# A fused transformer step in FP32: x loaded in natural rows, side work moved to other steps, other groups in the down projection

## Chip, core and metric

The kernel runs on one core of a Trainium2 chip. The metric is the device time of one execution in microseconds (us); the time of a version is the median of its runs.

## What is computed

One layer of a backbone for 512 latent tokens (a grid of 8 rows by 64 columns) and 128 context tokens, model width 2048, all in FP32. Cut to what matters here:

```python
sh1, sc1, g1, sh2, sc2, g2 = adaln(cond, w_ada, b_ada)       # silu(cond) @ w_ada: 2048 x 12288
h = modulate(rms_norm(x, norm1_g), sh1, sc1)
q, k, v, u = mixer_inputs(h, w_in, q_g, k_g)                  # one projection, 2048 x 4096
attn = neighbourhood_attention(q, k, v, cache_k, cache_v, rpb) # context tokens: dense attention
pool = multiscale_pool(u, w_pool, pool_scale)
x = x + g1 * merge_project(attn, pool, oa_g, op_g, w_out)     # 2048 x 2048
h = modulate(rms_norm(x, norm2_g), sh2, sc2)
x = x + g2 * swiglu(h, w_gate, w_up, w_down)                  # 2048 x 5632 twice, 5632 x 2048
```

Outputs are both kinds of tokens after the layer, and the context's new keys and values.

## The kernel before

**Layout.** The 640 tokens (latent first, then context) lie along the free dimension, features along the partitions. Inside the kernel the latent tokens are ordered by grid column, the 8 rows of a column next to each other. Every FP32 product is three matmuls of split operands: a value is `hi` (rounded for the fast FP32 mode) plus `lo` (the rest), and hi·hi, hi·lo and lo·hi are added.

**Start (to L683).** Five tiles of 128 tokens are loaded token by token (L259); `token_ap` gathers the latent ones in column order, so that neighbouring partitions are 64 tokens apart in memory. ScalarE (ACT) squares each tile, and VectorE (DVE) scales it. `turn` transposes one column block of 128 features on TensorE (PE) into PSUM, whence ACT writes `h_hi` and DVE `h`; GpSimd (POOL) makes `h_lo`. Meanwhile the value part of the input projection runs in blocks of one or two such column blocks, `starts`, in ten groups of matmuls each. The shift and scale of the first modulation are worked out beside it: `ada_stream` is a generator that loads a 1 MB piece of `w_ada` and multiplies it each time it is called; `next(stream)` after a group calls it once, `ada_until(b)` until block b is done. It has three buffers.

**Steps.** All other projections are cut into 688 steps. In a step a 256 x 256 tile of weights is multiplied by seven products in place of eight (a Strassen-like scheme of sums of quarters): 21 matmuls of 320 or 322 columns, into seven PSUM banks. `step` (L410) issues, for step s: `fetch(s+4)`, the weights' DMA on SyncE's queue (SP), into one of three buffers; `sums(s+3)`, the quarters' sums, on POOL; `x_hi(s+2)` on ACT and `x_lo(s+2)` on DVE, the split; then the jobs that `at((s, 0), ...)` registered for the step, the 21 matmuls (`products`), and the jobs of `(s, 1)`. At the end of a block `combine` (L397) adds the seven banks into an output tile: one copy on ACT (L401), seven additions on DVE (L400). The engines' queues run in program order, so a job stands ahead of all that is issued after it. In the last step of a block the split of step s+2 stands behind `combine`.

**Output projection.** 8 blocks of 8 steps. `x2_block` adds the gated result to x (DVE), stores it (SP) and sums its squares (ACT, POOL); `h2_block` scales it for the second norm (ACT) and stores it; `x_load` fetches the next x. The last block and the first gate block are ordered by a planner.

**Gate and up.** 22 pairs of 256 features, each a gate block and an up block of 8 steps. After a gate block: `scale_rho` (DVE, L1642), `gate` (ACT Silu, L1647). After an up block: `scale_rho`, `add_shift` (ACT), `times` (DVE, L1630), `f_sums` (DVE), and `f_split`, which splits seven operand tiles (ACT L1670, DVE L1671) and stores them to DRAM (`yh_s`, `yl_s`): four sums in step 3 after the block and three given quarters in step 6. Over the first nine blocks `ada_gen` works out the last modulation: groups of matmuls in steps 0 and 4, its transposes (L753) one step after ACT's copy (L749).

**Down.** The 22 pairs are taken in `GROUPS`, and within a group all 8 output blocks run, one step per pair; a result is added to `acc` in SBUF after each block (`accumulate`, DVE, L1769). The operands of a group are loaded back by `y_load` (four DMAs a pair, L1699) into 7 places; `late_loads` loads those whose place is not free before the group's last block. `start_sum` loads x for the sums. In the last group `finish` transposes two output blocks (PE, L1781) into one PSUM bank, copies and stores them; `finish_end` does the last two blocks behind the last step.

## Time and profile before

| | us |
|---|---|
| median of three runs | 2852.61 (2847.11 to 2853.16) |
| the profiled execution | 2848.62 |
| its span | 2846.8 |
| PE busy | 2628.8 (92%) |
| POOL busy | 1892.4 (66%) |
| DVE busy | 1872.0 (66%) |
| ACT busy | 1084.7 (38%) |

The span is the time from the first to the last event of the profiled execution. Busy times of engines overlap. A view of windows lists, for each stretch, the busy time of each engine with its count of instructions, the granted clock of PE as a share of full speed, the share of the DMA engines and the rate. In a list of instructions the brackets tell how long the engine was idle before one, and what ended that.

### The profile page before, as it was taken

To read this page: it belongs to the slowest core of one execution; us is meant where nothing else is said; L and a number is where in the kernel's file an instruction comes from. 1 tells how busy PE (TensorE), PEld (TensorE's weight loads), DVE (VectorE), ACT (ScalarE), POOL (GpSimd) and SP (SyncE) were. 2 spreads that over 40 slices of the span, in tenths; PEclk is the share of its full clock that TensorE was granted. 3 is DMA by queue.
4 is the path that set the end of the run, shared out by engine and by line. 5 is a ranking of instruction groups with operands and counts; after the bars stand their busy time and mean duration, and the time that the engine had idled before them with its cause. 6 is when DMAs were issued, how large, how long until landed. Compare 5 with 4: busy or idle time off the path is not lost. (4 is left out here: it accounts for less than half of the span.)

```text
span 2846.8 us, 46427 instructions
## 1 busy us (share of the span) xinstructions
PE 2628.8 (92%) x16968; PEld 2437.1 (86%) x16968; DVE 1872.0 (66%) x2580; ACT 1084.7 (38%) x1603; POOL 1892.4 (66%) x2265
## 2 busy tenths in 40 slices
PE   4997999988869977999999999999999989999998
PEld 2476988887668877888999999999999889998998
DVE  2469443458875587666676776776766778776765
ACT  3233222246633434434344444444444423332333
POOL 1257656567667867666677777676767568786764
PEclk9998999989989988999999999999999999999999
DMA  9922777768335443565344343343443765636343
GB/s 246 349 90 92 243 261 259 255 188 242 97 116 192 139 145 114 180 213 164 113 133 130 113 142 118 114 147 114 133 128 111 274 233 186 207 109 221 132 146 109
DMA packets 365142, 476.69 MB, mean 167 GB/s; under 512 B 22000, under 2 KB 286960, under 8 KB 364272
## 3 DMA queue, kind: packets, MB, share of 16 engines
q1 hardware_dynamic: 362752, 469.78, 50.9%
q10 hardware_dynamic: 2160, 3.93, 0.4%
q8 instruction: 133, 2.18, 0.3%
q14 instruction: 97, 0.79, 0.1%
HBM read 389.09 MB, written 84.54 MB: 166 GB/s over the span
## 5 line engine op out<-in xcount | busy, mean ns | idle before, releaser
L320 POOL TENSOR_TENSOR wf<-wf 128x128 f32<-128x128 f32 (+1 forms) x2007 | 1564.2, 786 | 670.6 <-DMA wf<-in_w_gate_dram 128.3
L393 PE MATMUL pp<-yhi,xhi 128*128 128x322 f32 (+1 forms) x4076 | 1285.8, 315 | 35.4 <-ACT c L401 14.9
L395 PE MATMUL pp<-yhi,xlo 128*128 128x322 f32 (+1 forms) x4076 | 1282.8, 315 | 23.7 <-DVE xlo L335 19.4
L394 PE MATMUL pp<-ylo,xhi 128*128 128x322 f32 (+1 forms) x4076 | 1273.4, 312 | 24.5 <-DMA ylo<-yl_s 10.0
L335 DVE TENSOR_TENSOR xlo<-wf,xhi 128x896 fp32r<-128x896 f32 x678 | 808.4, 1202 | 702.0 <-ACT xhi L329 669.7
L329 ACT CAST xhi<-wf 128x896 fp32r<-128x896 f32 x688 | 646.0, 941 | 1093.6 <-POOL wf L320 934.9
L393 PEld LDWEIGHTS pp<-yhi,xhi 128*128 128x128 f32 x4076 | 778.7, 191 | 67.1 <-DVE c L400 18.6
L395 PEld LDWEIGHTS pp<-yhi,xlo 128*128 128x128 f32 x4076 | 778.4, 191 | 40.2 <-DVE xlo L335 36.0
L394 PEld LDWEIGHTS pp<-ylo,xhi 128*128 128x128 f32 x4076 | 778.3, 191 | 27.2 <-DMA ylo<-yl_s 11.3
L400 DVE TENSOR_TENSOR c<-c,pp 128x320 f32<-128x320 f32 (+1 forms) x714 | 312.1, 484 | 85.3 <-ACT c L401 57.2
L393 PE MATMUL pp<-hhi,xhi 128*128 128x320 f32 x384 | 124.8, 325 | 0.2 <-DVE v L674 0.2
L394 PE MATMUL pp<-hlo,xhi 128*128 128x320 f32 x384 | 121.4, 316 | 0.0
L395 PE MATMUL pp<-hhi,xlo 128*128 128x320 f32 x384 | 121.4, 316 | 0.0
L394 PE MATMUL pp<-tlo,xhi 128*128 128x320 f32 x288 | 92.5, 321 | 16.7 <-DVE tlo L637 16.7
L393 PE MATMUL pp<-thi,xhi 128*128 128x320 f32 x288 | 91.2, 317 | 1.3 <-DVE v L674 1.3
L674 DVE TENSOR_TENSOR v<-g,v 128x512 f32<-128x512 f32 x80 | 54.9, 688 | 56.9 <-PE g L166 56.9
L395 PE MATMUL pp<-thi,xlo 128*128 128x320 f32 x288 | 91.5, 318 | 0.0
L393 PEld LDWEIGHTS pp<-hhi,xhi 128*128 128x128 f32 x384 | 74.6, 194 | 19.1 <-issue 13.4
L160 POOL TENSOR_TENSOR wlo<-raw,whi 128x512 fp32r<-128x512 f32 x32 | 41.3, 1312 | 69.9 <-ACT whi L159 68.3
L1671 DVE TENSOR_TENSOR c<-c,yh 128x640 f32<-128x640 f32 x88 | 82.3, 975 | 0.0
L1626 ACT ACTIVATE c<-c 128x320 f32<-128x320 f32 x132 | 50.6, 462 | 75.5 <-DVE c L1642 75.4
L1647 ACT ACTIVATE c<-c 128x320 f32<-128x320 f32 x132 | 52.9, 464 | 66.5 <-DVE c L1642 66.5
(238 smaller groups left out, 2586.5 us busy)
## 6 DMA issues: line engine op xcount, KB each, us to landing
araw<-in_w_ada_dram SPq DMA_DIRECT2D x60, 1024.0 KB, 6.7
wf<-in_w_gate_dram SPq DMA_DIRECT2D x176, 256.0 KB, 2.8
wf<-in_w_up_dram SPq DMA_DIRECT2D x176, 256.0 KB, 3.0
wf<-in_w_down_dram SPq DMA_DIRECT2D x176, 256.0 KB, 2.8
araw<-in_w_ada_dram SPq DMA_DIRECT2D x56, 512.0 KB, 7.0
wf<-in_w_in_dram SPq DMA_DIRECT2D x96, 256.0 KB, 4.3
yl_s<-c SPq DMA_DIRECT2D x66, 320.0 KB, 4.3
wf<-in_w_out_dram SPq DMA_DIRECT2D x64, 256.0 KB, 3.0
```

What stands on the lines that cost most here:

```text
L160: nc.gpsimd.tensor_tensor(lo, raw, hi.bitcast(F32), op=ALU.subtract)
L320: tt = lambda o, a, b, op: eng.tensor_tensor(o, a, b, op=op)
L329: nc.scalar.copy(hi, raws[s][:, 0:7, :])
L335: eng.tensor_tensor(lo, f[:, 0:7, :], hi.bitcast(F32), op=ALU.subtract)
L393: mm(b, lhsT=x[0][:, i, :], rhs=y[j][0], start=first, stop=False)
L394: mm(b, lhsT=x[0][:, i, :], rhs=y[j][1], start=False, stop=False)
L395: mm(b, lhsT=x[1][:, i, :], rhs=y[j][0], start=False, stop=last)
L400: add = lambda o, a, b: nc.vector.tensor_tensor(o, a, b, op=ALU.add)
L674: nc.vector.tensor_tensor(dst, ps, dst, op=ALU.add)
L1626: nc.scalar.activation(cq[:, c0:c1], cq[:, c0:c1], AF.Identity, bias=b)
L1647: nc.scalar.activation(cq[:, c0:c1], cq[:, c0:c1], AF.Silu, bias=b)
L1671: nc.vector.tensor_tensor(v, v, hi.bitcast(F32), op=ALU.subtract)
```

## The change

`x` is loaded in natural rows, and the reordering of tokens is done by the reading side of `turn`. All start blocks have two column blocks; the modulation stream is called from the first block on. In the output projection the two tiles of `x2_block` are handled in two steps, `h2_block` comes two steps later, and `x_load` one. In gate/up the gate's `scale_rho` and Silus come one step later, `f_split` works on one tile at a time (sums in step 3, given quarters in steps 9 and 10, that is 1 and 2 of the next up block), and the modulation generator runs in steps 2 and 6. The down groups have 4, 5, 4, 5, 4 pairs, loads and accumulations have other steps, and the ends of the last blocks are written anew. The core of the diff:

```diff
-    nc.sync.dma_start(c_s, c4)          # now behind the first ada_until
-    def turn(kt):
+    def turn(kt, eng=nc.gpsimd):
+        by_column = lambda v: v.rearrange("p (c r) -> p c r", r=ROWS)
...
+            if s == 0:
+                src = ps_s.rearrange("p (r c) -> p c r", r=ROWS)
+                to = [by_column(v[:, 0:SMP]) for v in (hi, h)]
+            else:
+                src, to = ps_p, [v[:, SMP:TOK] for v in (hi, h)]
+            nc.scalar.activation(to[0], src, AF.Identity, bias=b, scale=g)
+            nc.vector.tensor_scalar(to[1], src, g, b, op0=ALU.mult, op1=ALU.add)
-    starts = [(0, 1), (1, 1)] + [(k, 2) for k in range(2, NKT, 2)]
+    starts = [(k, 2) for k in range(0, NKT, 2)]
-        nc.sync.dma_start(xn[t], token_ap(x_sample, x_prompt, t, 0, D))
+        nc.sync.dma_start(xn[t], x_prompt if t == NT - 1 else x_sample[t * P : (t + 1) * P, :])
-    GROUPS = ((0, 3), (3, 7), (7, 12), (12, 17), (17, 22))
+    GROUPS = ((0, 4), (4, 9), (9, 13), (13, 18), (18, 22))
     turn(0)
+    turn(1, nc.vector)
-                if b:
-                    next(stream, None)
+                next(stream, None)
...
     def x2_block(j, c):
         for q in range(2):
-            x2_add(j, c, q)
-            nc.sync.dma_start(x2_s[2 * j + q], c[q][:, 0:TOK])
-        for q in range(2):
+            at((now[0] + q, 0), x2_tile, j, c, q)
+    def x2_tile(j, c, q):
+        x2_add(j, c, q)
+        at((now[0], 1), lambda: nc.sync.dma_start(x2_s[2 * j + q], c[q][:, 0:TOK]))
...
-            if n == 3:
+            if n == 4:
                 x_load(j)
-        at((now[0], 0), x2_block, j, c)
+        x2_block(j, c)
         if j < 6:
-            at((now[0] + 2, 0), h2_block, j, c)
+            at((now[0] + 4, 0), h2_block, j, c)
...
+    def f_split(pair, first, v):
+        n = v.shape[1]
+        hi = rhop.tile([P, 2, HB], F32R, tag="yh", name="yh", bufs=2)[:, 0:n, :]
+        nc.scalar.copy(hi, v)
+        nc.vector.tensor_tensor(v, v, hi.bitcast(F32), op=ALU.subtract)
...
-            at((first + 1 + 2 * i // 3, 1), y_load, p, part)
+            at((first + 1 + max(3 * i // 5, i // 4), 1), y_load, p, part)
...
-                    if ada_gen is not None:
-                        run_at(ada_gen, n % 4 == 0)
+                    if ada_gen is not None and n % 4 == 2:
+                        next(ada_gen, None)
-                at((now[0] + 3, 0), split_f_sums, sg, pair)
-                at((now[0] + 6, 0), split_f_given, c, pair)
+                later = 4 if pair == NPAIR - 1 else 9
+                for i in range(2):
+                    at((now[0] + 3, i), split_f_sums, sg, pair, i)
+                    at((now[0] + later + i, 0), split_f_given, c, pair, i)
-                at((now[0], 0), scale_rho, sg)
-                at((now[0], 1), gate, sg, 0)
-                at((now[0] + 1, 1), gate, sg, 1)
+                at((now[0] + 1, 0), scale_rho, sg)
+                at((now[0] + 1, 1), gate, sg, 0)
+                at((now[0] + 2, 1), gate, sg, 1)
...
-                at((now[0], 0), accumulate, j, c)
+                at((now[0] + (2 if gi == 0 else 0), 0), accumulate, j, c)
-            if last_group and j % 2 and j < 7:
+            if last_group and j in (1, 3, 5, 6):
                 for t in range(NT):
-                    at((now[0] + 2 + t, 1), finish, j - 1, t)
-    finish_end(6)
-    accumulate(7, c)
-    finish_end(7)
+                    at((now[0] + 1 + (t > 1), 1) if j == 6 else (now[0] + 2 + t, 1), finish, (j - 1, j)[j == 6 :], t)
+    finish_end(7, ps)
```

The new `finish_end` takes the seven banks in the order in which the last step fills them (0, 6, 1, 2, 4, 3, 5), adds, gates and accumulates quarter by quarter on DVE, and sends the five output tiles over SP's and ACT's queues. In the first group the early loads begin at step 8 and `start_sum` two to five steps later than before.

## Rows read from the trace of the kernel before

**Rows 1.** Windows, two stages: length; each engine's busy time, count; clock, DMA share, GB/s.

```profile
1108.40:2248.20 1139.80, 1116.87 (x7370) 1079.77 (x7370) 781.21 (x948) 482.19 (x733) 796.38 (x1027) 0.99 0.44 141
2248.20:2836.40 588.20, 561.48 (x3759) 554.37 (x3759) 421.38 (x627) 193.82 (x240) 408.58 (x523) 0.98 0.52 175
```

**Rows 2.** Windows, two stretches of the start, same columns.

```profile
45.00:50.00 5.00, 5.00 (x24) 3.57 (x26) 0.00 (x0) 2.92 (x6) 0.19 (x1) 1.00 0.01 2
50.00:147.00 97.00, 86.22 (x486) 43.82 (x474) 39.02 (x75) 20.48 (x37) 25.88 (x19) 0.98 1.04 337
```

**Rows 3.** Waits of PE: who waited for whom: us in total, times, longest.

```profile
PE pp L395 <- DVE xlo L335: 19.4, 25, 3.5
PE pp L394 <- DMA ylo<-yl_s: 10.0, 5, 3.1
PE pp L393 <- DVE c L400: 9.8, 23, 1.3
PE x L753 <- ACT rest L749: 9.2, 4, 2.6
```

**Rows 4.** Timeline of ACT, 0 to 29 us: start, length, what, idle before.

```profile
18.95 1.91 ACT L265 ACTIVATE junk<-x 128x2048 bf16<-128x2048 f32 x1 [3.50 <-DMA x<-in_x_sample_dram]
23.77 1.91 ACT L265 ACTIVATE junk<-x 128x2048 bf16<-128x2048 f32 x1 [2.82 <-DMA x<-in_x_sample_dram]
26.23 1.91 ACT L265 ACTIVATE junk<-x 128x2048 bf16<-128x2048 f32 x1 [0.45 <-DMA x<-in_x_prompt_dram]
```

**Rows 5.** Timeline of PE: the last modulation matmuls of the start.

```profile
145.92 1.07 PE L203 MATMUL acc<-araw,c 128*32 128x512 f32 x8
```

**Rows 6.** Groups of DVE instructions: count; busy us, mean ns; idle before.

```profile
L239 DVE TENSOR_SCALAR c<-ps_s,gs,sh 128x512 f32<-128x512 f32 x16 | 13.0, 809 | 23.9 <-ACT hhi L238 20.9 <-POOL wlo L160 1.9 <-POOL hlo L240 1.1
L219 DVE TENSOR_REDUCE red<-tr 128x8 f32<-128x32 f32 x7 | 1.3, 181 | 0.0
L219 DVE TENSOR_REDUCE red<-tr 128x4 f32<-128x16 f32 x2 | 0.3, 174 | 17.2 <-PE tr L217 17.2
```

**Rows 7.** Timeline of POOL in the output projection: two additions of squares.

```profile
902.82 3.20 POOL L1502 TENSOR_TENSOR c<-c,xT 128x640 f32<-128x640 f32 x2 [1.66 <-ACT xT L1501]
```

**Rows 8.** Windows: an up block, the shortest block, the last 34 blocks.

```profile
1494.61:1520.63 26.02, 25.70 (x171) 24.89 (x169) 16.16 (x23) 10.94 (x16) 21.21 (x28) 1.00 0.41 128
1935.05:1959.93 24.88, 24.88 (x171) 24.86 (x169) 18.64 (x23) 11.38 (x18) 15.68 (x21) 1.00 0.40 127
1366.95:2248.17 881.22, 868.18 (x5715) 849.01 (x5713) 621.02 (x747) 379.50 (x577) 634.49 (x811) 1.00 0.41 132
```

**Rows 9.** Timeline of DVE around the ends of an up and a gate block.

```profile
1467.44 3.20 DVE L400 TENSOR_TENSOR c<-c,pp 128x322 f32<-128x322 f32 x7 [0.58 <-ACT c L401]
...
1492.94 1.76 DVE L1671 TENSOR_TENSOR c<-c,yh 128x640 f32<-128x640 f32 x2
1494.62 3.19 DVE L400 TENSOR_TENSOR c<-c,pp 128x322 f32<-128x322 f32 x7
...
1500.44 1.55 DVE L1642 TENSOR_TENSOR c<-c,rho 128x640 f32<-128x640 f32 x2
...
1505.29 1.28 DVE L335 TENSOR_TENSOR xlo<-wf,xhi 128x896 fp32r<-128x896 f32 x1 [0.53 <-ACT xhi L329]
```

**Rows 10.** Timeline of PE: the first matmul of that up block's fifth step.

```profile
1508.14 0.31 PE L393 MATMUL pp<-yhi,xhi 128*128 128x322 f32 x1
```

**Rows 11.** Windows: the first down group (24 steps) and the second (32).

```profile
2248.17:2344.32 96.15, 81.98 (x506) 77.05 (x505) 78.24 (x122) 30.33 (x43) 53.61 (x74) 0.95 0.75 259
2344.32:2442.97 98.65, 98.65 (x675) 98.35 (x673) 80.90 (x121) 33.28 (x41) 81.06 (x96) 1.00 0.52 174
```

**Rows 12.** Timeline of SP: the weight fetch in the third down step.

```profile
2258.64 0.38 SPq L314 DMA_DIRECT2D wf<-in_w_down_dram  x1
```

**Rows 13.** One line, L1699 (y_load): from issue to landing.

```profile
DMA to landing us min/median/max: 3.8/5.8/9.8
```

**Rows 14.** Timeline of SP: the last five output stores.

```profile
2841.15 3.13 SPq L1808 DMA_DIRECT2D out_dram<-ylo  x5
```

More of the change, by code (lines that the diff above doesn't have):

```diff
@@ L408, in combine, with step @@
         add(c[0], c[0], p2)
-    def step(ps, y, first, out, order=range(7)):
+    def step(ps, y, first, out, order=range(7), last=False):
         s = now[0]
@@ L419, in step @@
             fn(*args)
-        products(ps, xs.pop(s), y, first, out is not None, order)
+        products(ps, xs.pop(s), y, first, last or out is not None, order)
         if out is not None:
@@ new lines, in finish_end, with plus, turns @@
+    def finish_end(j, ps):
+        c = [c_tile(2 + q)[:, 0:TOK] for q in range(2)]
+        p1, p6, p5, p7, p3, p4, p2 = ps
+        c11, c12, c21, c22 = quarters(c, HB)
+        add = lambda o, a, b: nc.vector.tensor_tensor(o, a, b, op=ALU.add)
+        trs = [psum.tile([P, HX], F32, tag="p", name="ytr", bufs=7)[:, 0:256] for t in range(NT)]
+        r3 = room().rearrange("p (t n) -> p t n", t=NT)
+        def plus(q, h, eng=nc.vector):
+            kt = 2 * j + q
+            for s, a, b in ((0, 0, HB),) if h == 0 else ((0, HB, SMP), (1, SMP, TOK)):
+                o = acc[kt][:, a:b]
+                eng.scalar_tensor_tensor(o, c[q][:, a:b], gate_c[5][:, kt, s : s + 1], o, op0=ALU.mult, op1=ALU.add)
+        def turns(q):
+            for t in range(NT):
+                src = acc[2 * j + q][:, t * P : (t + 1) * P]
+                nc.tensor.transpose(trs[t][:, q * P : (q + 1) * P], src, ident)
+        nc.scalar.copy(c11, p1)
+        add(c22, c11, p6)
+        add(c11, c11, p2)
+        plus(0, 0)
+        add(c12, c22, p5)
+        add(c12, c12, p3)
+        plus(0, 1)
+        add(c21, c22, p7)
+        add(c22, c21, p5)
+        turns(0)
+        plus(1, 1)
+        add(c21, c21, p4)
+        plus(1, 0)
+        turns(1)
+        for t in (2, 3, 4, 0, 1):
+            (nc.scalar.copy if t % 2 else nc.vector.tensor_copy)(r3[:, t, :], trs[t])
+            eng = nc.scalar if t % 2 else nc.sync
+            eng.dma_start(token_ap(y_sample, y_prompt, t, j * 256, 256), r3[:, t, :])
```

68 lines of the change are left out of this document (26 added, 42 removed).

## The prediction

> **How I read it.** I took the stages first [rows 1]: TensorE (PE) is the busy engine in each, and what an edit is worth is how long PE stands idle or slowed there. PE is 98% busy in the gate/up stage and 95% in the down projection, together 1728 of the 2847 us, and 89% in the start from 50 to 147 us, where DMA is at its full share [rows 2]. Next the list of whom PE waits for [rows 3], which holds only the waits between a matmul and its releaser; then the length of single blocks against the shortest of their kind, which also shows what many waits of some tenths add up to; and for each kind of late block the lane of the engine that is late. No stage is bound by one thing. The start is bound by DMA up to 147 us [rows 2, 4, 5]; gate/up and down by PE with VectorE (DVE) as the engine that is late at block ends; the first down block by DMAs that are issued late. The sum below is made against the profiled execution: 2846.8 us of span, 2848.6 in all. The three runs before have a median of 2852.6, 4.0 above it, so I add half of that, 2, to what comes out.
>
> **Start: x in natural rows, all blocks of two, the stream from the first block on.** ACT squares each x tile when it lands. The third and fourth sample tiles land 4.82 us apart, the prompt tile, whose rows follow each other in memory, 2.46 us after the fourth [rows 4]. All are 1 MB in rows of 8 KB; the sample tiles alone are gathered with a step of 64 rows, 512 KB. In natural rows I price each at 2.46: x is in at 26.2 - 4 x (4.82 - 2.46) = 16.8 us, 9.4 earlier (2.46, as the prompt, and 4.82, no change, are the bounds; I take the prompt, since the pattern in memory is then the same). From there to 147 us the queue moves 337 GB/s [rows 2] and the last modulation matmuls run at 145.92 [rows 5]. Up to then 33.5 MB of w_ada and 4 MB of w_in pass whatever the order, 111 us. Before, the transfers stood still from 45 to 50 us [rows 2], because the first block asked the stream for nothing; now each of its groups asks, though with three buffers a pause of 3 to 5 us is left while the first group waits for its operands. The single-column blocks move 512-byte rows at a lower rate; blocks of two gain 2 us. So the stream ends 9.4 + 2 + (5 - 4) = 12 us earlier, 16 if nothing is left of the pause. What follows its end is the same as before; ten vacc additions fall away on DVE, which is not late there. I take **15**, near the upper end, since the first three loads find free buffers and go out right behind x.
>
> The other side of natural rows: ACT and DVE read the transposed tile out of PSUM with a step of 64 elements. A 512-wide DVE read takes 809 ns now, and no row has so long a strided one; the nearest read 16 and 32 elements, each 32 apart, in 174 and 181 ns [rows 6], so 16 more cost 7 ns. I price it at nothing, with twice the time as the other bound: 0.8 us on each of ACT and DVE, which follow one another on the one buffer, so 1.6 us in those 7 blocks whose second turn already waits, 11 us. The Trainium skill (Advanced Engine Details and Errata, Memory Cachelines) speaks for that bound: PSUM is read in lines of two FP32 values, and neighbours should be contiguous for full rate. The 7 ns speak against it, though on very short reads. By it the start would gain 4 in place of 15.
>
> A second page bears on the first step. The Trainium skill (DMA: Bandwidth & Descriptors, Latency and other measured facts) gives 207 GB/s at a row pitch of 512 KiB against 214 at full rate, 3%. By it x would be in less than 1 us earlier, and the start would gain 6. The spacing of the arrivals, 4.82 against 2.46 us, decides for me.
>
> **Output projection: one tile a step.** The two tiles' square sums on POOL, 3.20 us in a row [rows 7], hold up the weight sums of the next step; PE's waits for xlo are 19.4 us, many of them in this stage [rows 3]. One addition a step lets the first weight sums through 1.6 us earlier, but POOL does the same work until two steps later, so the later waits stay. x_load behind step 4 and h2 two steps later stand on SP ahead of fetches that have room. Between 0 and 8; I take **3**.
>
> **Gate/up: the large term.** A block is 8 steps of 21 matmuls. The shortest takes 24.88 us, an up block typically 26.02, and the 34 blocks behind the modulation stream 881.2 in all, 25.92 each [rows 8]: 35 us over 34 x 24.88. The lane shows why. At the end of an up block DVE starts to add the seven banks (L400) at 1467.44, 2 us before the next block's first matmul at 1469.41. At the end of a gate block it is still splitting the previous pair (L1671, 1.76 us from 1492.94), starts at 1494.62, and the next block begins at 1494.61: its banks are not free [rows 9]. PE's many short waits for L400 (9.8 us, 23 times [rows 3]) are these; the rest is spread over the two steps after. The split moves to steps 9 and 10, scale_rho (1.55 us [rows 9]) to 9 and the Silus to 9 and 10. What they now meet there: in step 9 and 10 DVE has two xlo (1.1 to 1.4 each), 1.76 + 1.55: 6.1 of 6.2 us. The xlo behind them is done at 1506.57 now (from 1505.29, 1.28 long [rows 9]), 1.6 us before its step, the block's fifth, begins at 1508.14 [rows 10]. I expect that to be used up and not passed. The stores, now eight DMAs a pair for six, go in the queue behind fetches two steps ahead. Of the 35 I take 31. In the first nine blocks the modulation stream adds 16 groups of 1.07 us [rows 5] and four sets of transposes, about 19 us in all, which stay; the transposes waited 9.2 us for ACT with others in the stage before [rows 3], some 8 of it here, and with the dip of the clock after them 14 us go (1108.4 to 1366.9 is 258.6 us for nine blocks, 224 + 19 + 15). With the stream in steps 2 and 6 the copy has four steps' time. Together **45**, between 30 and 50.
>
> **Down projection.** 588.2 us [rows 1] for 176 steps; the first group of four pairs takes 98.65 for 32 steps [rows 11], 3.08 each, with nothing lost. So 46 us are lost in all: 22.3 in the group of three (96.15 for 24 steps), where DVE has a combine and an accumulation to do in 9.2 us, 24 in the others, most of it where a group of five follows a group of five and its third and later pairs come late: PE's five waits for ylo, 10.0 us [rows 3], and the dips after them, and in the last group's transposes, 6 to 7. With 4, 5, 4, 5, 4 only two pairs are loaded late and each has the three steps that cost the one such transition there is now about 1 us: 4 to 5 us for four transitions. The first group has DVE room (the second's rate shows it), with accumulations just ahead of a combine: 3 us. But its fourth pair's last part is queued in the third step (`max(3*i//5, i//4)` is 9 for i = 15) and read in the fourth. The fetch of that step leaves SP at 2258.64 [rows 12], 10.5 us after the first down matmul at 2248.17, since it waits for an xlo behind scale_rho and the shifts; the load goes out 0.4 later and takes 3.8 to 5.8 us [rows 13]; PE reads it at 9.6. **New wait: 5 to 7 us**, and the clock's dip after it 2: 8 (0 if the load overtakes, 12 at most). The transposes of the last group stay (6.6), those of tile 6 now stand in line for one bank with copies and DMA issues of ACT between, 5. Together 46 - (8 + 3 + 5 + 12) = **18**, between 8 and 28. At the very end ten issues of 0.6 us on SP, the last five 3.13 us [rows 14], become three there and two on ACT, but DVE's chain is two pieces longer: **1**.
>
> **Sum.** 15 + 3 + 45 + 18 + 1 = 82; 2848.6 - 82 = 2766.6, with the 2 for the median **2769 us**.
>
> **Rivals.** (a) The wait moves and doesn't go: steps 9 and 10 cost each up block what the transition cost. For it, DVE has 0.1 us to spare there; against it, the two steps after are nearly empty. The 31 are lost: 2800. (b) x is no faster in natural rows, or the strided reads cost double: 9 to 11 lost, 2779. (c) The first down block doesn't wait, because its xlo comes earlier: 2761. (d) Slower than before: three weight buffers make a ring (xlo frees a buffer, then fetch, sums on POOL, xhi, xlo), and a late xlo in step 9 comes back three steps later as a late fetch. If both visits cost PE all 3.3 us of the moved work, 6.6 us in 22 pairs, 145 us: 2914. It decides from 3.8 us a pair on (84 us over 22). Against it: the 1.6 us [rows 10] that an xlo is early now. (e) The bank waits have another cause than the split, and nothing moves in gate/up or down beyond the modulation stream: about 2850.
>
> **Chances.** The forecast 0.57, (a) 0.12, (b) 0.15, (c) 0.11, (d) 0.03, (e) 0.02. The range reaches from (c) with a better start and gate/up (2746) to just short of (a) (2797). A measurement of this kernel tells 0.2%, 5.7 us, from no change: faster 0.95, same 0.02, slower 0.03.
>
> **What would show it.** Right: the prompt tile is squared at 17 us and the last modulation group runs near 131; up blocks take 25.0, and L400 starts 1 us or more before the next block in both kinds; no transposes (L753) wait for ACT; one wait of 5 us or more for ylo in the fourth down step. Wrong: up blocks of 26 with waits for xlo in their third to fifth step; sample tiles still 4.8 us apart; ACT's and DVE's reads in the turns at 1.5 us.

## The result

| | before | changed |
|---|---|---|
| median, us | 2852.89 (4 runs, 2847.11 to 2859.10) | 2828.97 (4 runs, 2823.79 to 2831.00) |
| the profiled execution, us | 2848.62 | 2829.12 |
| its span, us | 2846.8 | 2827.3 |

The ratio is 0.9913, with an interval of 0.9888 to 0.9938: the change takes 24 us away, where the forecast was 2769 (84 less) and the range began at 2746 and ended at 2797. The direction was right, the size was not: between the two profiles 19.5 us went of the 82 of the sum.

The stages of the changed kernel, in windows with the columns of [rows 1], from the first step of one stage to that of the next: the start, the attention and pooling stage, output blocks 13 to 18, the first nine gate and up blocks, the other 34, the first down group, and all of down.

```profile
0.00:204.96 204.96, 171.74 (x849) 104.77 (x849) 94.39 (x160) 63.05 (x100) 78.12 (x67) 0.99 0.74 248
...
583.52:782.11 198.59, 165.34 (x971) 139.40 (x970) 145.86 (x328) 113.12 (x233) 123.88 (x126) 0.86 0.61 179
828.91:1007.47 178.56, 162.30 (x1046) 150.36 (x1045) 91.22 (x112) 65.44 (x90) 125.29 (x148) 0.99 0.46 157
1109.04:1351.35 242.31, 242.31 (x1637) 227.62 (x1637) 160.96 (x200) 102.59 (x155) 166.43 (x211) 1.00 0.56 179
1351.35:2229.25 877.90, 863.03 (x5735) 845.72 (x5733) 632.55 (x747) 381.87 (x578) 652.43 (x811) 1.00 0.43 134
2229.25:2352.03 122.78, 108.43 (x673) 102.16 (x673) 85.80 (x128) 37.40 (x49) 75.39 (x99) 0.96 0.68 238
2229.25:2816.14 586.89, 565.38 (x3767) 552.37 (x3766) 426.88 (x628) 195.01 (x245) 427.74 (x525) 0.99 0.53 178
```

And three stages of the kernel before that its rows ahead do not show, in the same view:

```profile
599.18:792.73 193.55, 157.62 (x972) 130.18 (x971) 145.17 (x328) 112.45 (x233) 126.08 (x126) 0.91 0.63 182
839.53:1007.55 168.02, 158.06 (x1047) 150.09 (x1045) 91.89 (x112) 65.79 (x90) 127.50 (x151) 0.99 0.51 167
1108.36:1366.95 258.59, 248.70 (x1658) 230.77 (x1657) 160.20 (x204) 102.69 (x156) 161.91 (x216) 0.99 0.53 174
```

Blocks are counted from 0 over all the steps: 0 to 11 are the input projection, 12 to 19 the output projection, 20 to 63 gate and up, 64 to 103 the down projection. Read with [rows 1, 8, 11], the length of each window gives the ledger in us (the kernel before's first step comes at 221.62, its last ends at 2836.43; the steps of a stage not shown are taken from PE's timeline in the same way):

| stage | predicted | measured | off by |
|---|---|---|---|
| start, to the first step | 15 | 16.7 | +1.7 |
| input projection, attention, block 12 | 0 | -6.0 | -6.0 |
| output projection from block 13 on, first gate block (13 to 20) | 3 | -11.3 | -14.3 |
| gate/up, next nine blocks (21 to 29) | 14 | 16.3 | +2.3 |
| gate/up, other 34 blocks (30 to 63) | 31 | 3.3 | -27.7 |
| down | 18 | 1.4 | -16.6 |
| tail | 1 | -0.8 | -1.8 |
| sum (before rounding) | 82 | 19.5 | -62.5 |

Whom PE waits for now (us in total, times, longest), to be read beside [rows 3]:

```profile
PE pp L402 <- DVE xlo L342: 35.9, 63, 3.4
...
PE pp L400 <- DVE c L407: 7.7, 15, 2.0
```

The waits for the banks (c L400 before, c L407 now) fell from 9.8 to 7.7 us over all stages, and 9.5 of the 9.8 had stood in the last 34 gate and up blocks, where none is left. The waits for xlo rose from 19.4 to 35.9, and in those 34 blocks from 1.9 to 13.7. That is the shape of the whole result: a wait went and another came.

### The profile page after: what moved, and what is told of

It is laid out like the page before. It is cut to its first block, busy times and chain, and to the rows that moved or that the text cites. A ratio compares the mean times of both kernels' runs of the same rounds, so it can differ in the third digit from the quotient of the medians.

```text
span 2827.3 us, 46418 instructions
## 1 busy us (share of the span) xinstructions
PE 2629.4 (93%) x16936; PEld 2432.8 (86%) x16936; DVE 1883.0 (67%) x2566; ACT 1087.5 (38%) x1605; POOL 1927.7 (68%) x2264
## 5 line engine op out<-in xcount | busy, mean ns | idle before, releaser
L327 POOL TENSOR_TENSOR wf<-wf 128x128 f32<-128x128 f32 (+1 forms) x2007 | 1603.4, 805 | 615.5 <-DMA wf<-in_w_up_dram 110.9
L402 PE MATMUL pp<-yhi,xlo 128*128 128x322 f32 (+1 forms) x4072 | 1281.9, 315 | 40.4 <-DVE xlo L342 35.9
L400 PE MATMUL pp<-yhi,xhi 128*128 128x322 f32 (+1 forms) x4072 | 1279.9, 314 | 25.8 <-ACT c L408 9.6
L400 PEld LDWEIGHTS pp<-yhi,xhi 128*128 128x128 f32 x4072 | 775.2, 190 | 55.2 <-DVE c L407 13.0
L407 DVE TENSOR_TENSOR c<-c,pp 128x320 f32<-128x320 f32 (+1 forms) x707 | 308.8, 484 | 48.7 <-ACT c L408 28.0
L400 PE MATMUL pp<-hhi,xhi 128*128 128x320 f32 x384 | 124.6, 325 | 3.1 <-DVE v L682 3.1
L400 PEld LDWEIGHTS pp<-hhi,xhi 128*128 128x128 f32 x384 | 74.3, 193 | 21.8 <-issue 12.6
L1653 DVE TENSOR_TENSOR c<-c,rho 128x640 f32<-128x640 f32 x88 | 92.7, 1092 | 0.0
L400 PE MATMUL pp<-thi,xhi 128*128 128x320 f32 x288 | 91.2, 317 | 0.2 <-ACT thi L637 0.2
L1678 ACT CAST yh<-c 128x640 fp32r<-128x640 f32 x88 | 58.0, 659 | 68.0 <-DVE c L1668 63.3
L1637 ACT ACTIVATE c<-c 128x320 f32<-128x320 f32 x132 | 50.8, 462 | 74.6 <-DVE c L1653 74.5
```

The lines of the kernel that those rows point to most:

```text
L327: tt = lambda o, a, b, op: eng.tensor_tensor(o, a, b, op=op)
L400: mm(b, lhsT=x[0][:, i, :], rhs=y[j][0], start=first, stop=False)
L402: mm(b, lhsT=x[1][:, i, :], rhs=y[j][0], start=False, stop=last)
L407: add = lambda o, a, b: nc.vector.tensor_tensor(o, a, b, op=ALU.add)
L1637: nc.scalar.activation(cq[:, c0:c1], cq[:, c0:c1], AF.Identity, bias=b)
L1653: nc.vector.tensor_tensor(v, v, xo.rho.rearrange("p (h n) -> p h n", h=2), op=ALU.mult)
```

## The experiments

The kernels e1 to e11 (there is no e7) are the changed kernel with one or more edits undone, moved or left out, e10 and e11 on top of e3, each run once; e12 puts edits together and is run five times. The runs of the changed kernel spread over 7 us, so I read an edit in the window of its own stage. Stages that an edit doesn't touch show the scatter: the 34 blocks with the changed kernel's gate and up code took 877.9, 878.1, 880.1, 881.0, 881.0, 882.3 and 882.5 us in seven kernels, output blocks 13 to 18 with the changed code 177.5 to 182.5. With the changed kernel's start the first step came at 204.96 us here and at 205.1 to 209.0 in the ten other kernels that have it.

### x and the start (e6)

```diff
-        nc.sync.dma_start(xn[t], x_prompt if t == NT - 1 else x_sample[t * P : (t + 1) * P, :])
+        nc.sync.dma_start(xn[t], token_ap(x_sample, x_prompt, t, 0, D))
```

(and `turn` reads and writes in order again)

> The changed kernel with x gathered by columns as before (rows 512 KB apart in memory) and turn's reads and writes contiguous; the blocks of two and the stream from the first block on stay. Theory 1: 9 to 10 us of the start's 16.3 come from x: the prompt tile is squared at 25 to 27 us in place of 16.2, the last modulation matmul ends at 139 to 142 in place of 130.7, and the whole is 2834 to 2840. Theory 2: the stream's end is set by its own transfers and blocks, and x earlier only shifts the pause: the end stays within 3 us of 130.7. The strided reads of PSUM cost nothing if ACT's and DVE's 512-wide reads take 778 and 809 ns here too.

ACT's squares of the last two x tiles in the changed kernel, and the last modulation group on PE (start, length, what, idle before):

```profile
13.62 1.91 ACT L272 ACTIVATE junk<-x 128x2048 bf16<-128x2048 f32 x1 [0.54 <-DMA x<-in_x_sample_dram]
16.16 1.91 ACT L272 ACTIVATE junk<-x 128x2048 bf16<-128x2048 f32 x1 [0.54 <-DMA x<-in_x_prompt_dram]
...
129.65 1.06 PE L202 MATMUL acc<-araw,c 128*32 128x512 f32 x8
```

and with x gathered by columns again, in e6:

```profile
22.93 1.91 ACT L268 ACTIVATE junk<-x 128x2048 bf16<-128x2048 f32 x1 [2.77 <-DMA x<-in_x_sample_dram]
25.37 1.91 ACT L268 ACTIVATE junk<-x 128x2048 bf16<-128x2048 f32 x1 [0.43 <-DMA x<-in_x_prompt_dram]
```

The natural rows come 2.54 us apart, the gathered ones 4.77 (from the third to the fourth), then the prompt tile 2.44. x is in 9.2 us later here, and the last modulation group ends at 139.7 for 130.7: 9.0 of the 16.3 us by which that group ends earlier than before (146.99, [rows 5]) are x alone, the forecast's 9.4. The first step comes at 213.94 in e6, 4.9 to 9.0 later than in the kernels with the changed start. The rest is put down to the stream asked from the first block on and the blocks of two; no run separates these.

The strided read costs nothing. Groups of the start in the changed kernel, with count, busy us and mean ns:

```profile
L244 ACT ACTIVATE hhi<-ps_s,sh,gs 128x512 fp32r<-128x512 f32 x16 | 12.5, 778 | 30.1 <-PE ps_s L233 30.1
...
L245 DVE TENSOR_SCALAR c<-ps_s,gs,sh 128x512 f32<-128x512 f32 x16 | 12.9, 809 | 22.8 <-ACT hhi L244 20.9 <-POOL wlo L159 1.9
```

DVE's read takes 809 ns, as the contiguous one in [rows 6]; ACT's takes 778, and 779 with the contiguous read of e6.

### The output projection (e1, e9)

> The changed kernel with the output projection's side work as before: both tiles of a block's result in one step, the scaling and the next x at their old steps. Theory 1: with one tile a step, the work runs twice round a loop of ACT and DVE in which each waits for the other in its queue: the split's xlo on DVE (1.7 us), the addition to x on DVE (1.4), its square on ACT (0.7), the next xhi on ACT (0.9), 4.7 us a step for 3.08. Undone, blocks 13 to 18 take 168 us as in the kernel before, in place of 178.6, and the whole 2818 to 2820. Theory 2: these blocks are late for another reason (the weights' fetches or the clock), and they stay at 178, the whole at 2829. The attention stage, which neither version touches, took 218.3 us before and 223.4 after with more of it at half clock: if that is chance, it lies anywhere between 217 and 225 here; if it comes from the earlier start, it stays at 223.

In e1 the diff's three places at `x2_block`, `x_load` and `h2_block` are turned back. Its window of blocks 13 to 18:

```profile
826.34:994.16 167.82, 157.82 (x1046) 150.11 (x1044) 90.17 (x112) 65.77 (x90) 129.50 (x151) 0.99 0.52 167
```

e9 leaves out one addition:

```diff
                 nc.scalar.activation(xo.xT[:, q, :], c[q][:, 0:TOK], AF.Square)
-                nc.gpsimd.tensor_tensor(xo.sumsq, xo.sumsq, xo.xT[:, q, :], op=ALU.add)
```

> The changed kernel without POOL's addition of the squares in the output projection (1.56 us a tile, the sum for the second norm then holds one tile only, so the values behind it differ; all else runs as before). In the changed kernel three steps of a block take 4.6 to 4.9 us for 3.08, and blocks 13 to 18 178.6 to 182. Theory 1: two of the three are bound by the loop of ACT and DVE (xlo 1.1 to 1.7, addition 1.4, square 0.7, xhi 0.9), which the POOL addition only slows by the 0.6 us that xlo takes longer beside it: these steps still take 4.1 to 4.4, and the six blocks 168 to 173. Theory 2: POOL is the bound (three sums of 0.9 to 1.0 us and an addition of 1.56 are 4.6 a step): without the addition the steps fall to 3.1 to 3.5 and the six blocks to 155 to 164.

```profile
827.40:992.24 164.84, 157.66 (x1046) 148.68 (x1045) 90.98 (x116) 65.17 (x90) 109.17 (x140) 1.00 0.52 171
```

Undone, blocks 13 to 18 are back at 167.8 us (168.0 before) and blocks 13 to 20 at 268.9 (268.8 before, 280.1 in the changed kernel), and the execution took 2815.1: the whole loss of 11.3 us is this edit, and the 3 of the forecast never came. One part of how, the changed kernel's timelines of DVE, ACT and POOL in block 14 show:

```profile
869.43 1.72 DVE L342 TENSOR_TENSOR xlo<-wf,xhi 128x896 fp32r<-128x896 f32 x1 [1.64 <-ACT xhi L336]
871.08 1.41 DVE L1494 SCALAR_TENSOR_TENSOR c<-c,g1c,xT 128x512 f32<-128x512 f32 x2
...
867.83 0.74 ACT L1511 ACTIVATE xT<-c 128x640 f32<-128x640 f32 x1 [2.56 <-DVE c L1494]
868.47 0.93 ACT L336 CAST xhi<-wf 128x896 fp32r<-128x896 f32 x1
872.52 0.74 ACT L1511 ACTIVATE xT<-c 128x640 f32<-128x640 f32 x1 [3.12 <-DVE c L1494]
873.19 0.94 ACT L336 CAST xhi<-wf 128x896 fp32r<-128x896 f32 x1
...
868.65 1.56 POOL L1512 TENSOR_TENSOR c<-c,xT 128x640 f32<-128x640 f32 x1 [1.66 <-ACT xT L1511]
```

ACT squares the first tile (867.83), then rounds xhi (868.47); DVE takes the rest of that, xlo (869.43), and only then adds the second tile to x (871.08); ACT's next square waits 3.12 us for it (872.52), and the next xhi (873.19) stands behind the square. One turn is 872.52 - 867.83 = 4.69 us, in a step of 3.08. Before, both tiles went through in one turn. POOL is in the loop as well: in blocks 13 to 18 every xlo that overlaps one of its additions takes 1.68 to 1.74 us, most others 1.1, and its weight sums start only behind the addition (870.16).

Average step lengths of output blocks 14 to 16, from the starts of their first matmuls (the sixth step holds 1.07 us of the modulation):

| step | 1 | 2 | 3 | 4 | 5 | 6 | 7 | 8 |
|---|---|---|---|---|---|---|---|---|
| before | 3.08 | 3.14 | 3.23 | 5.61 | 3.53 | 4.15 | 3.18 | 3.06 |
| changed | 4.20 | 3.25 | 3.79 | 4.72 | 4.59 | 4.86 | 3.18 | 3.06 |
| side work as before | 3.08 | 3.08 | 3.25 | 5.43 | 3.60 | 4.15 | 3.18 | 3.06 |
| no additions on POOL | 3.80 | 3.45 | 3.62 | 4.27 | 4.03 | 4.15 | 3.18 | 3.06 |

Without POOL's additions the two steps of the loop still take 4.27 and 4.03, about as the first theory said, and the sixth step's excess of 0.7 is gone, as the second said; the six blocks, 164.8 us, lie just outside both. So one slow step of 5.6 us was traded for two of 4.6 to 4.7, by the loop of ACT and DVE, a sixth that is 0.7 longer, by POOL's arrears, and a third that is 0.6 longer.

The first step's 4.20 is another matter. It is block 14 alone, 6.43 (3.08 in blocks 15 and 16), and the last step of block 13 ahead of it takes 4.54 in place of 3.06: 4.8 us in all, none in the kernel before and in e1, 2.6 to 5.4 in every other kernel with this edit. ACT and SP in block 13 of the changed kernel:

```profile
853.95 1.02 ACT L1519 ACTIVATE c<-c,gs 128x512 f32<-128x512 f32 x2 [5.63 <-DMA x_s<-c]
...
848.25 0.81 SPq L1488 DMA_DIRECT2D xT<-x_s  x2
...
849.58 0.47 SPq L1505 DMA_DIRECT2D x_s<-c  x1
```

The scaling of `h2_block` (L1519) overwrites the tile that the store of `x2_tile` (L1505) sends, and waits 5.63 us for it, with two xhi and the copy of the next combine behind it on ACT. The store leaves SP only at 849.58: it stands behind `x_load` (L1488), which waits 5.6 us until POOL's addition has read its buffer (848.2), and behind a fetch. Only in block 13 does `h2_block` come in the same step as that store; later it comes two steps behind it and doesn't wait. So 4.8 of the 10.7 us by which blocks 13 to 18 differ from e1 come from a store behind a load; the rest is in the third to sixth steps above.

### Gate and up (e2, e3, e10, e11)

> The changed kernel with the gate and up side work (scaling, Silu, splits and stores) at the steps of before; the modulation stream stays in steps 2 and 6. Theory 1: moving the splits only moved the wait, from the block's end to the fifth step of the up block, so the last 34 blocks take about 881 us as before in place of 878, and the whole is 2829 to 2835. The first nine blocks (242 us after, 259 before) owe their gain to the stream's steps and stay within 6 us of 242. Theory 2: the move did bring the 31 us of the forecast and something else in the changed kernel took them back: then the 34 blocks take 900 us or more here.

In e2 the diff is turned back at `f_split`, `split_f_sums`, `split_f_given` and at the lines that register them, `scale_rho` and `gate`. Its first nine and its other 34 blocks:

```profile
1109.37:1354.85 245.48, 243.50 (x1638) 227.61 (x1637) 158.25 (x202) 103.33 (x155) 169.52 (x213) 1.00 0.56 177
1354.85:2236.09 881.24, 866.50 (x5735) 846.81 (x5734) 616.88 (x748) 380.18 (x578) 638.75 (x812) 1.00 0.43 134
```

The 34 blocks take 881.24 us, what they took before (881.22) and within the scatter of the changed code (877.9 to 882.5): the moved side work brings nothing that the scatter lets one see. It does move the waits: with the old steps PE waits 11.0 us for the banks in these blocks and 3.1 for xlo, in the changed kernel not at all for the banks and 13.7 for xlo. The first nine keep 13.1 of their 16.3 us, so those belong to the modulation's steps. Average steps of the last 32 blocks, in us. The columns count a block's steps from 1; the steps of the jobs in the text count from 0 behind the end of the gate or up block that they follow, so that "step 9" behind an up block is the second column of the next up block:

| | 1 | 2 | 3 | 4 | 5 | 6 | 7 | 8 | block |
|---|---|---|---|---|---|---|---|---|---|
| before, gate | 3.10 | 3.11 | 3.09 | 3.11 | 3.15 | 3.24 | 3.45 | 3.16 | 25.40 |
| before, up | 4.39 | 3.41 | 3.10 | 3.09 | 3.12 | 3.13 | 3.13 | 3.11 | 26.48 |
| changed, gate | 3.10 | 3.13 | 3.09 | 3.21 | 3.14 | 3.50 | 3.46 | 3.12 | 25.76 |
| changed, up | 3.12 | 3.21 | 3.10 | 3.17 | 3.86 | 3.13 | 3.13 | 3.11 | 25.83 |
| e3, gate | 3.13 | 3.14 | 3.10 | 3.22 | 3.18 | 3.38 | 3.47 | 3.14 | 25.75 |
| e3, up | 3.17 | 3.27 | 3.10 | 3.10 | 3.12 | 3.13 | 3.26 | 3.26 | 25.40 |
| e10, gate | 3.10 | 3.12 | 3.09 | 3.09 | 3.12 | 3.13 | 3.13 | 3.25 | 25.03 |
| e10, up | 4.20 | 3.40 | 3.10 | 3.09 | 3.12 | 3.13 | 3.16 | 3.17 | 26.37 |
| e11, gate | 3.14 | 3.15 | 3.10 | 3.09 | 3.12 | 3.26 | 3.26 | 3.12 | 25.23 |
| e11, up | 3.13 | 3.18 | 3.09 | 3.09 | 3.12 | 3.13 | 3.21 | 3.26 | 25.21 |

The 1.27 us of the up block's first step are gone, and 0.74 stand in its fifth, 0.26 more in the gate block's sixth. The timelines of an up block of the changed kernel, DVE, ACT and PE:

```profile
1487.80 1.36 DVE L1679 TENSOR_TENSOR c<-c,yh 128x640 f32<-128x640 f32 x1
1489.08 2.08 DVE L1653 TENSOR_TENSOR c<-c,rho 128x640 f32<-128x640 f32 x2
...
1490.19 1.21 ACT L1658 ACTIVATE c<-c 128x320 f32<-128x320 f32 x3 [3.12 <-DVE c L1653]
1491.30 0.92 ACT L336 CAST xhi<-wf 128x896 fp32r<-128x896 f32 x1
...
1493.40 0.42 PE L402 MATMUL pp<-yhi,xlo 128*128 128x322 f32 x1 [0.56 <-DVE xlo L342]
```

ACT's Silu (L1658) waits 3.12 us for scale_rho (L1653), which DVE starts only after the moved split; the xhi of the fifth step stands behind the Silu in ACT's queue (1491.30), its xlo behind that, and PE waits.

The wait itself is not new. ACT in the up block of [rows 9], in the kernel before:

```profile
1501.29 1.20 ACT L1647 ACTIVATE c<-c 128x320 f32<-128x320 f32 x3 [3.24 <-DVE c L1642]
```

There it stands in the block's second step, in all 17 up blocks of the 34, and holds up the xhi of the fourth: its xlo, done at 1504.75, is 0.3 us ahead of its step at 1505.05. The change moved the wait two steps on and put the split ahead of what it waits for.

```diff
-                at((now[0] + 1, 0), scale_rho, sg)
+                at((now[0], 0), scale_rho, sg)
```

> The changed kernel with one line moved: the gate's scale_rho in step 8 in place of 9, the Silus where they are. Theory 1: the wait of 0.9 us in the up block's fifth step comes from ACT's queue: xhi stands behind a Silu that waits for scale_rho on DVE. With scale_rho a step earlier the Silu waits for nothing, the up blocks fall from 25.5 to 25.0 us, and the whole by 8 to 13 us, to 2816 to 2821. Theory 2: DVE itself has no room in these steps (6.1 of 6.2 us), whatever the order; then the wait stays or goes to the block's first steps, and the whole is within 4 us of 2829.

```profile
1489.54 1.20 ACT L1658 ACTIVATE c<-c 128x320 f32<-128x320 f32 x3
```

The Silus (1489.54) run right behind the cast ahead of them, the fifth step is at 3.12 again, the up blocks at 25.40 (25.10 without the last one, block 63). The 34 blocks take 871.1, 7 to 11 less than with the changed code; the whole took 2827.0, since other stages fell on the slow side of their scatter (output blocks 13 to 18 at 182.2).

```diff
-                at((now[0], 1), add_shift, c)
-                at((now[0] + 1, 0), times, c, sg)
-                at((now[0] + 2, 0), f_sums, sg, c)
+                at((now[0] + 1, 1), add_shift, c)
+                at((now[0] + 2, 0), times, c, sg)
+                at((now[0] + 3, 0), f_sums, sg, c)
...
-                    at((now[0] + 3, i), split_f_sums, sg, pair, i)
+                    at((now[0] + 4, i), split_f_sums, sg, pair, i)
```

> The kernel of e3 (scale_rho of the gate in step 8) with the up block's shift on ACT, and times, f_sums and the first splits behind it, each one step later. Measured for e3: up blocks 25.40, gate blocks 25.75 us each, the last 34 blocks 871.1. Theory 1: the gate blocks lose their 0.9 us the same way as the up blocks did: the shift waits on ACT for scale_rho on DVE (3.7 us idle), two xhi stand behind it, and the delay comes out in the sixth and seventh step. With the shift a step later the gate blocks fall to 25.0 to 25.3, the 34 blocks to 860 to 865. Theory 2: DVE's work in the gate block (scale_rho, times, f_sums, splits, 9.9 us with its xlo beside it) is what delays, whatever ACT waits for: gate blocks stay at 25.6 to 25.9, or the delay moves to the block's end.

```profile
1510.35 2.30 ACT L1637 ACTIVATE c<-c 128x320 f32<-128x320 f32 x6 [0.48 <-DVE c L1653]
...
1530.76 0.43 ACT L408 COPY c<-pp 128x322 f32<-128x322 f32 x1 [4.30 <-DMA yl_s<-c]
```

The shift waits 0.48 us instead of 3.7, and the gate blocks fall to 25.03. But the copy that opens the gate block's combine now waits 4.30 us for the store of the split sums, whose tile it overwrites (2.4 on average, in 12 of the 17 gate blocks); the next up block pays 1.1 us in its first step. The 34 blocks are at 875.0. That points to the order of the shift as the cause of the gate block's loss, and to the late store as the price of this way of moving it; four jobs moved here, and e11 separates them.

```diff
-                at((now[0], 1), add_shift, c)
-                at((now[0] + 1, 0), times, c, sg)
+                at((now[0] + 1, 0), add_shift, c)
+                at((now[0] + 1, 1), times, c, sg)
```

(on the kernel of e3)

> The kernel of e3 with the up block's shift on ACT moved only behind the next xhi, and times behind that step's xlo; f_sums and the splits stay where they are, so the stores are not later. With everything a step later (e10) the gate blocks took 25.03 us, but the copy that opens the gate block's combine waited 4.3 us for a store of the splits, and the up blocks took 26.37. Theory 1: ACT's order is the cause, and the late stores were e10's own price: here gate blocks take 25.0 to 25.3, up blocks stay at 25.3 to 25.5, and the 34 blocks fall to 858 to 864 (871.1 in e3, 877.9 to 882.5 in the others). Theory 2: whatever frees the gate block's sixth step moves the wait to the next block's start, since the ring of three weight buffers has no room: the two kinds together stay at 51.0 to 51.4 a pair, as in e3 (51.15) and e10 (51.40).

```profile
1350.94:2210.59 859.65, 855.90 (x5734) 848.17 (x5733) 645.03 (x749) 384.14 (x578) 698.21 (x812) 1.00 0.44 138
```

Both kinds of blocks at 25.2, 859.7 us in all: the first theory, with the up blocks even a little better. With both jobs placed so that ACT hardly waits with an xhi behind it (the Silu not at all, the shift 0.54 us in 5 of 17 blocks), 21.6 of the forecast's 31 us are there, against the kernel before. What is left above 24.88 a block, 0.3, I did not follow.

### The first down group (e4, e5, e8)

The changed kernel's fourth down step, on PE and on SP, and DVE at the end of block 66:

```profile
2248.35 0.63 PE L401 MATMUL pp<-ylo,xhi 128*128 128x320 f32 x1 [6.12 <-DMA ylo<-yl_s]
...
2242.92 0.38 SPq L321 DMA_DIRECT2D wf<-in_w_down_dram  x1
2243.35 0.46 SPq L1702 DMA_DIRECT2D ylo<-yl_s  x1
...
2280.39 1.74 DVE L1774 SCALAR_TENSOR_TENSOR ylo<-ylo,g2c 128x512 f32<-128x512 f32 x2
2282.05 3.16 DVE L407 TENSOR_TENSOR c<-c,pp 128x320 f32<-128x320 f32 x7
```

PE waits 6.12 us for the last load, which SP issued at 2243.35, behind a fetch that waited for an xlo; this is the new wait of the forecast (5 to 7). Below it, the accumulation (3.4 us from 2278.77 on, its second half shown) stands right ahead of the combine, which starts at 2282.05.

```diff
-            at((first + 1 + max(3 * i // 5, i // 4), 1), y_load, p, part)
+            at((first + 1 + (i // 2 if early else max(3 * i // 5, i // 4)), 1), y_load, p, part)
...
-    late_loads(last_up, range(GROUPS[0][1]))
+    late_loads(last_up, range(GROUPS[0][1]), True)
```

(the third argument is `early`)

> The changed kernel with the 16 loads of the first down group queued at two a step, so that the last goes out two steps earlier. Theory 1: the load issued 5 us before it lands is what the fourth down step waits for (6.1 us and a dip of the clock behind it); earlier by two steps it lands in time, the first down block takes 16 to 17 us in place of 24.0, and the whole 2820 to 2823. Theory 2: SP waits for buffers of the weights anyway, and the loads ahead take the transfers' time from the weights' fetches: the block stays above 21 us, with the wait at the weights.

The first block of the group, and the seven behind it:

```profile
2228.63:2247.22 18.59, 16.14 (x84) 14.09 (x85) 14.20 (x18) 5.96 (x10) 12.72 (x17) 0.91 0.83 306
2247.22:2351.53 104.31, 95.30 (x591) 89.35 (x590) 72.82 (x110) 31.40 (x39) 60.99 (x84) 0.97 0.65 221
```

The wait for the load is gone and the first block is at 18.59 for 24.00, but the group is at 122.90 for 122.78: the seven blocks behind it take 104.3 for 98.8. (In the seven kernels that edit neither loads nor accumulations of this group its first block took 20.6 to 23.6 us, the seven behind it 98.4 to 101.3 and the group 121.1 to 123.8.) DVE at the end of e4's first block, and PE's first matmul there that waits for it:

```profile
2246.72 2.23 DVE L1668 TENSOR_TENSOR c<-c,c 128x320 f32<-128x320 f32 x3
2249.05 0.97 DVE L1679 TENSOR_TENSOR c<-c,yh 128x640 f32<-128x640 f32 x1
2249.95 3.18 DVE L407 TENSOR_TENSOR ylo<-ylo,pp 128x320 f32<-128x320 f32 x7
...
2250.47 0.64 PE L400 MATMUL pp<-yhi,xhi 128*128 128x320 f32 x1 [1.28 <-DVE ylo L407]
```

DVE goes without a pause from f_sums (L1668) through a split to the combine (L407), PE has ended the block at about 2248 and waits for the banks; block 65 takes 16.7 for 12.3. In the changed kernel DVE has the same f_sums and split there (2246.33 to 2249.99), but PE, held up by the load, ends its products later still, and the combine, at 2250.16, waits for PE. Neither theory had that.

```diff
-                at((now[0] + (2 if gi == 0 else 0), 0), accumulate, j, c)
+                at((now[0], 0), accumulate, j, c)
```

(and the loads of x for the sums two to five steps earlier)

> The changed kernel with the first down group's accumulations at the first step of the next block, as before, in place of the third, and the loads of x for them two to five steps earlier. In the changed kernel the blocks 65 to 71 take 100.8 us, 14.7 above 7 x 12.3. Theory 1: the accumulation on DVE (1.9 to 3.3 us) stands right ahead of the combine and makes it late; at the first step it has room, as in the second group before, whose blocks of four lost nothing. The blocks 68 to 71 fall to 12.3 to 12.6 each, the seven by 8 to 12 us, the whole to 2817 to 2821. Theory 2: the loads of x stand ahead of weight fetches, or the accumulation delays the next xlo: the seven stay within 4 us of 100.8.

```profile
2232.89:2259.52 26.63, 16.34 (x86) 14.65 (x85) 17.64 (x27) 8.47 (x14) 14.10 (x21) 0.81 0.72 260
2259.52:2352.47 92.95, 88.63 (x590) 86.25 (x589) 74.17 (x107) 30.26 (x37) 61.04 (x78) 1.00 0.68 233
```

The seven blocks lose 92.95 - 86.2 = 6.7 us for 12.5, and those from the fifth on take 12.3 to 13.7: 5.8 of the 8 to 12 expected, by the stage's own window in the changed kernel (98.8; the 100.8 of the expectation was too high by 2). That is outside both theories, and clear of the scatter. The first block is 2.6 longer, 26.63, so that the group gains 3.2, and the whole, 2829.4, has gained nothing.

> The changed kernel with three edits in the first down group: the 16 loads at two a step, the accumulations at the first step of the next block, and the splits and stores of the last pair (which no group needs before the last) in steps 5, 6, 9 and 10 in place of 3 to 5. With the loads alone the first block fell from 24.0 to 18.6 us and the group stayed at 122.9, because the next blocks lost what it gained (16.7 and 16.1 for 12.3). Theory 1: DVE has a backlog there, from f_sums, the splits, a combine and an accumulation in a row, and ACT waits 3 to 7 us for a store to free a split's buffer; with the splits out of the way the first three blocks take 15 to 16, 13 and 13 us, and the group 103 to 108. Theory 2: the backlog comes from scale_rho, the shift and times of the last up block, which stay: the first three blocks still take over 48 us, and the group only gains what the accumulations give, 8 to 12.

```diff
-                later = 4 if pair == NPAIR - 1 else 9
+                a, b = ((9, 10), (5, 6)) if pair == NPAIR - 1 else ((3, 3), (9, 10))
                 for i in range(2):
-                    at((now[0] + 3, i), split_f_sums, sg, pair, i)
-                    at((now[0] + later + i, 0), split_f_given, c, pair, i)
+                    at((now[0] + a[i], i if a[0] == 3 else 0), split_f_sums, sg, pair, i)
+                    at((now[0] + b[i], 0), split_f_given, c, pair, i)
```

```profile
2228.18:2342.10 113.92, 105.69 (x673) 100.25 (x674) 90.47 (x133) 38.66 (x51) 77.16 (x99) 0.99 0.70 245
```

The group is at 113.9, 8.9 less than in the changed kernel, between the two theories (103 to 108; 111 to 115), nearer the second: the first three blocks take 17.0, 16.3 and 12.8, 46 us together. That fits a backlog of DVE of which a part (scale_rho, times and f_sums of the last pair) stayed; three edits are in this run, and none isolates that part.

### Together (e12)

> The changed kernel with what the runs point to: the output projection's side work as before (10.8 us in e1), the gate's scale_rho in step 8 and the shift behind the next xhi, the first down group's loads at two a step, its accumulations at the first step, and of the last pair f_sums in step 5, the given quarters' splits in step 6, the sums' in 9 and 10. If the gains add up, since they lie in different stages: 2829 less 11 for the output projection, 9 to 20 for gate and up, 10 to 15 for the first down group, 2784 to 2799. If each frees only what the next wait takes, as the loads alone did in e4, it is 2810 or more. The time of the kernel before is 2844 to 2853.

The output projection's side work as before, scale_rho and the shift as in e11, the loads and sums of e8, and of the last pair f_sums in step 5, the given quarters' splits in step 6, the sums' in 9 and 10. Windows of blocks 13 to 18, the 34 blocks, and the first down group:

```profile
828.74:998.58 169.84, 159.63 (x1046) 151.57 (x1044) 91.14 (x112) 65.77 (x90) 128.04 (x151) 0.98 0.51 165
1342.95:2204.34 861.39, 856.98 (x5735) 849.14 (x5733) 647.51 (x750) 384.19 (x578) 697.54 (x814) 1.00 0.44 138
2204.34:2315.94 111.60, 103.84 (x674) 98.89 (x674) 90.06 (x130) 38.62 (x51) 75.65 (x97) 1.00 0.71 244
```

The median of five runs is 2788.88 us (2785.57 to 2791.79), 0.9788 of the kernel before in the same rounds (2850.00; 0.9773 to 0.9804), 40 us below the change as it was made. The gains lie in different stages and add up: of the 37.3 us between its profile and that of the changed kernel, 8.7 + 16.5 + 11.2 = 36.4 are in these windows.

## Why the prediction was wrong

**Start: right, and a little lucky.** x came in at 16.2 us for 16.8 forecast, the last modulation group ended at 130.7 for 131, the strided reads were free, and the start gained 16.7 for 15. The other ten kernels with this start gain 12.6 to 16.5, so the profile shown is the best of them. What followed the start took 6.0 us back, for which the sum had no term. 5 of them lie in attention and pooling, where no instruction is changed: the granted clock (a mean over stretches at 1.2 and at 2.4 GHz) is 0.86 there and was 0.91. With the last steps of the input projection this stage took 223.3 us, 217.5 to 223.1 in the eleven experiments, which leave it alone too, and 218.3 before. Up to block 13 this kernel is 10.6 us ahead of the kernel before, the ten others with its start 10.7 to 15.9. So the 5 us are within what the same code does from run to run. An effect of the earlier start isn't excluded: the three kernels whose first step came earliest (204.96, 205.13 and 206.05 us) have the longest attention stages (223.3, 223.1 and 222.6), though the fourth (206.44) has the shortest, and 218.3 is a single profile. The cause stays open.

**Output projection: wrong in sign.** The step that failed is "POOL does the same work until two steps later, so the later waits stay": it looked at POOL alone. Without POOL's additions the six blocks take 164.8 us, with them and the old order 167.8, with them and the new order 178.6. The tile's path runs DVE, ACT, POOL, and on DVE and ACT it stands between the splits of two steps. One tile a step sends the path and the split round each other twice. All could have been read from the trace before, where the addition, the square and the two halves of the split each have a length; I added them up for one engine only. A second step failed beside it, "x_load behind step 4 and h2 two steps later stand on SP ahead of fetches that have room": x_load also stands ahead of the second tile's store, for which ACT's scaling waits 5.63 us in block 13, and 4.8 us of the loss are there.

**Gate/up, first nine blocks: right** (16.3 for 14; no wait of L753's transposes is left; e2 gives the modulation's steps 13.1).

**Gate/up, the other 34: rival (a), which had 0.12.** The bank waits had the cause that the forecast gave: they went, and they are back in e2 (11.0 us). The failed step is "I expect that to be used up and not passed": the 1.6 us by which xlo is early [rows 10] were held against DVE's 6.1 us of work. One xlo was looked at, the fifth step's, and not ACT, where the Silu waited 3.24 us for scale_rho already. The Silu was moved too; it still waits for scale_rho and holds up the xhi behind it, so the path was split 1.36, half of scale_rho 1.04, Silu 1.21, xhi 0.92, xlo 1.09, 5.6 us one behind the other on two engines, though neither engine was full. Where the forecast wrote "DVE has 0.1 us to spare" it had counted an engine's load, and not a path over two queues. e3 and e11 show it: the same work, in an order in which ACT hardly waits, takes 859.7 in place of 877.9.

**Down: 1.4 for 18.** The new wait was right in place, cause and size: 6.12 us, and 8.35 with the dip behind it (a granted clock of 0.58 from 2248.35 to 2253.25), for 8. The same block lost 3.3 more, mostly in its first and third steps (4.57 and 4.76 us for 3.08), for which the sum had no term. The transitions took 7.0 of loss for 5, the last group 13.6 for 12. The failed term is "The first group has DVE room (the second's rate shows it), with accumulations just ahead of a combine: 3 us": blocks 65 to 71 lost 12.5. The room of the second group before [rows 11] was taken as proof, though there the accumulations stood at the first step of a block and no last pair was being split. e5 shows the place of the accumulation at work (12.5 to 6.7). That the rest is the backlog of the last pair is what e4 and e8 point to; it is not isolated.

**Tail: -0.8 for 1**, within what one profile can tell.

Rival (d), a late xlo that comes back round the ring of weight buffers, does not show as a loss: up blocks average 25.83 us for 26.48. Rival (e) was added up wrong: without the 31 of the other gate/up blocks and the 18 of down, 33 of the 82 us are left, which makes 2818 us and not about 2850. The measured 2829 lies near that, but not for its reason, since the bank waits did come from the split. Rival (a) accounts for 28 of the 62 us that were missing; the output projection's 14 and down's 17 are as much again.

## What to carry to other kernels

A job on an in-order queue costs not its own time but the time until its operand is there, for all that stands behind it. Before moving a job, write the path across the engines in order, with the critical work that stands behind each of its pieces, and compare its length with a step; engine load says little. When a wait is taken away, ask who had been catching up during it: the loads made earlier in e4 gained 5.4 us in one block and lost 5.5 in the next seven.

## What was unexpected in the hardware

512-wide reads of a transposed tile out of PSUM with a step of 64 elements took 778 ns on ACT and 809 on DVE, as long as contiguous ones. The Trainium skill (Advanced Engine Details and Errata, Memory Cachelines) lets one expect a cost for other than contiguous pairs; for these two engines and this step the runs show none.

Tiles of 1 MB in rows of 8 KB land every 4.77 us with the rows 512 KB apart (in runs of eight) and every 2.5 us one behind the other. The Trainium skill (DMA: Bandwidth & Descriptors, Latency and other measured facts) gives 3% for this pitch in copies with 16 KiB rows, all at one pitch; here it is a factor of 1.9, and in e6 the last modulation group ends 9 us later for it.

DVE's xlo, with two operands in SBUF, took 1.09 us in most steps. In output blocks 13 to 18 of the changed kernel it took 1.68 to 1.74 wherever it met one 640-wide addition on POOL, in e1 2.42 to 2.46 beside two in a row. In e9, without the additions, it took 1.62 to 1.65 three times beside the weight sums alone, so the addition is not the only thing on POOL that goes with a longer xlo.
